# Attention's steps in TensorE's hand-written order begin at S5 block 3's transposes in place of block 1's

## The chip, the cores and the metric

The kernel runs as one launch on one core of a Trainium2 chip. The metric is the device time of one execution in microseconds (us); three executions of the kernel before took 1083.37, 1087.34 and 1088.72 us, median 1087.34. About 0.5% is what a measurement of this kernel can tell from no change.

## The reference, cut to what matters

One encoder layer over 2048 tokens of width 1024. A combined input projection feeds two mixers that run side by side:

```python
proj = x @ s5_w_in                          # 512 columns for S5, 256 for the queries
mix = _s5_mixer(proj[..., :512], ...)       # 32 groups of 16 channels, 64 complex states each,
                                            # a scan over tokens forward and one backward,
                                            # y -> g = gelu(y) -> g * sigmoid(g @ w_glu + b_glu)
mem_out = _memory_attention(proj[..., -256:], mem, w_kv)   # 4 heads of 64, 256 memory tokens, softmax
y = concat([mix, mem_out]) @ w_out
x = LN(alpha * x + y);  x = LN(alpha * x + MoE(x))          # 16 experts, 2 per token
```

The change is in the stretch where the S5 outputs and the attention over the memory tokens are computed; the GLU (`g @ w_glu`) follows, then the output projection, then the mixture of experts.

## The kernel before, in words

**Stages.** `front` computes the projections (`inproj_u`), then the S5 scans and outputs and the attention, then `glu`, then `outproj`; `moe` follows. Tokens are treated in 16 tiles of 128. The 32 S5 groups are treated in 8 blocks of four; the scans of the blocks run in the order 6, 7, 0, 1, 2, 3, 4, 5, mostly on VectorE and GpSimd (`turn_states`, L690 to L695, and the scan itself, L715), and ScalarE copies a scanned block into `SS` (L720).

**The S5 outputs.** `s5_out(b)` does for block b four groups of eight float32 matmuls each: `U` against `M` (L802, L803), `SS` against `wol` (L804, L805). Two groups share one PSUM tile `py`, which ScalarE copies to `gt` (L807). `M` and `wol` are loaded through SP's queue for each pair of groups (L789, L796). After every odd block come four sets of four transposes (`trg`, L816) of two blocks' outputs; each set fills a PSUM tile and is passed through `gelu`: ScalarE Square (L824), VectorE (L825), ScalarE Tanh (L826), VectorE (L827), the last of which writes `gT` (named S in the rows) and is the last reader of the `trg` tile. `py` and `trg` share one ring of three PSUM tiles (pool `ps1`, tag "s5"); `gu`, the scratch of `gelu`, has two buffers.

**The attention.** `attention_steps` is a generator of 57 steps: in round n (0 to 18) it does `att_values(n - 3)`, `att_probs(n - 2)` and `att_scores(n)`, where these tiles exist, one per step. `att_scores` is eight matmuls into `pS` (two PSUM tiles, L734, L735), a maximum on VectorE (`nm`, L737), four exponentials on ScalarE into `pe` (L740), a reciprocal (L742) and a multiply on GpSimd (L743). `att_probs` transposes `pe` (L757) and splits it into `th` (ScalarE, L758) and `tl` (VectorE, L759). `att_values` is 24 small matmuls (L773). The SBUF pool of `pe` (`attw`) is opened where the pool of the scans' scratch tiles `R` and `m` was closed before, and the pool of the GLU's `gh` and `gl` is opened where `attw` was closed: a tile waits until the last user of the memory beneath it is done.

**The order on TensorE.** Around the S5 outputs TensorE's order is that of the program (`manual_schedule`); the order on the other engines is planned by the framework. `s5_out` yields ahead of each group and ahead of each set of transposes, 48 times in all: blocks 0, 2, 4, 6 four times, blocks 1, 3, 5, 7 eight times (four groups, four sets). At each yield the next number of `STEPS` says how many attention steps are issued there:

```python
with self.tc.manual_schedule(engines={mybir.EngineType.PE}):
    counts = iter(STEPS)
    for b in range(NB):
        if b == GELU:
            self.glu_weights()
        for _ in self.s5_out(b, gtp, wp, gup):
            for _ in range(next(counts)):
                next(steps, None)
    for _ in steps:
        pass
```

Before, `STEPS` is `(0,) * 8 + (1,) + (2,) * 39`: none at the groups of blocks 0 and 1, one at the first set of transposes behind block 1, two at every yield after that until the 57 steps are used up, which is in block 6.

Of the kernel before, what the change touches and what calls it, by code (L numbers as in the profile page):

```python
# [50 lines left out]
SPLIT = 1024  # L51
WHOLE_T = 12
BATCHES = ((0, 4), (4, 4), (8, 2), (10, 2), (12, 2), (14, 2))
STEPS = (0,) * 8 + (1,) + (2,) * 39
ATL = (2, 3)
WIP = 3
LW = 4
# [15 lines left out]
class Kern:  # L73
# [97 lines left out]
    def front(self, fr):  # L171
# [17 lines left out]
        with ExitStack() as s5:  # L189
# [9 lines left out]
            with ExitStack() as t2:  # L199
# [17 lines left out]
# [3 lines that stand above are left out]
# [1387 lines left out]
```

## Time and profile before

| what | value |
|---|---|
| median of three executions | 1087.34 us |
| the profiled execution | 1077.7 us |
| its span in the trace | 1075.9 us |
| TensorE matmul busy | 896.7 us (83%) |
| VectorE busy | 825.0 us (77%) |
| ScalarE busy | 540.8 us (50%) |
| GpSimd busy | 537.4 us (50%) |
| mean granted TensorE clock | 0.931 |
| TensorE busy in 440 to 490 us (GLU) | 48.66 of 50 us |
| TensorE busy in 490 to 520 us (output projection's start) | 29.48 of 30 us |

A profile page gives the share of busy time of each engine over the span, and the trace gives each instruction with its start, its duration and what ended the idle time ahead of it. Times in the rows are microseconds from the start of the span. PE is TensorE, DVE VectorE, ACT ScalarE, POOL GpSimd, SP the queue that issues most transfers. PEclk 1.00 is the upper of TensorE's two clock levels (2.4 GHz), 0.50 the lower (1.2 GHz). The stretch of the change reaches from about 290 to 440 us of the span; the GLU's first matmul (tile `pg`) starts at 440.12.

### The profile page before, as it was taken

To read this page: it belongs to the slowest core of one execution; us is meant where nothing else is said; L and a number is where in the kernel's file an instruction comes from. 1 tells how busy PE (TensorE), PEld (TensorE's weight loads), DVE (VectorE), ACT (ScalarE), POOL (GpSimd) and SP (SyncE) were. 2 spreads that over 40 slices of the span, in tenths; PEclk is the share of its full clock that TensorE was granted. 3 is DMA by queue.
4 is the path that set the end of the run, shared out by engine and by line. 5 is a ranking of instruction groups with operands and counts; after the bars stand their busy time and mean duration, and the time that the engine had idled before them with its cause. 6 is when DMAs were issued, how large, how long until landed. Compare 5 with 4: busy or idle time off the path is not lost. (4 is left out here: it accounts for less than half of the span.)

```text
span 1075.9 us, 18762 instructions
## 1 busy us (share of the span) xinstructions
PE 896.7 (83%) x7108; PEld 607.8 (56%) x7108; DVE 825.0 (77%) x1636; ACT 540.8 (50%) x1068; POOL 537.4 (50%) x379
## 2 busy tenths in 40 slices
PE   7778599986754999899999988599959996988980
PEld 4445465675643777444555557486647664755640
DVE  7999988969997676384486866379858787978874
ACT  5122253445748777477743421366636564745530
POOL 1475755426664332324946364524544566357554
PEclk9899899999886999999999996899989999999995
DMA  7113355275171422326755341675568669658431
GB/s 258 40 44 119 122 181 200 70 234 188 48 226 43 154 80 80 120 77 244 252 177 80 121 116 62 246 294 192 199 239 306 214 227 341 216 193 286 170 96 66
DMA packets 65198, 178.14 MB, mean 166 GB/s; under 512 B 15120, under 2 KB 33424, under 8 KB 57680
## 3 DMA queue, kind: packets, MB, share of 16 engines
q1 hardware_dynamic: 44800, 128.83, 36.5%
q0 software_dynamic: 20304, 48.07, 12.9%
q8 instruction: 57, 0.93, 0.4%
q14 instruction: 37, 0.30, 0.1%
HBM read 141.95 MB, written 58.49 MB: 186 GB/s over the span
## 5 line engine op out<-in xcount | busy, mean ns | idle before, releaser
L92 DVE SCALAR_TENSOR_TENSOR wl<-raw,wh 128x1024 f16<-128x1024 f32 x82 | 97.7, 1219 | 10.1 <-ACT wh L91 10.1
L91 ACT ACTIVATE wh<-raw 128x1024 f16<-128x1024 f32 x82 | 82.0, 1048 | 23.3 <-PE pg L109 12.2
L109 PE MATMUL pg<-xl,wh 128*128 128x288 f16 (+1 forms) x256 | 72.4, 285 | 5.1 <-DVE xl L1477 4.4
L108 PE MATMUL pg<-xh,wh 128*128 128x288 f16 (+1 forms) x256 | 72.8, 286 | 2.9 <-ACT xh L1476 1.8
L1221 POOL DMA_INDIRECT xs<-xg,idxall x31 | 39.4, 1272 | 71.4 <-DVE xg L1514 41.9
L108 PE MATMUL pu<-xh,wh 128*128 128x288 f16 (+1 forms) x256 | 72.1, 284 | 1.9 <-DVE hl L1063 1.9
L110 PE MATMUL pg<-xh,wl 128*128 128x288 f16 (+1 forms) x256 | 72.1, 284 | 0.5 <-issue 0.5
L110 PE MATMUL pu<-xh,wl 128*128 128x288 f16 (+1 forms) x256 | 72.0, 284 | 0.0
L109 PE MATMUL pu<-xl,wh 128*128 128x288 f16 (+1 forms) x256 | 71.9, 284 | 0.0
L109 PEld LDWEIGHTS <-wh 128*128 128x128 f16 x576 | 58.1, 101 | 20.6 <-issue 7.1
L110 PEld LDWEIGHTS <-wl 128*128 128x128 f16 x576 | 57.9, 101 | 20.0 <-issue 6.8
L108 PEld LDWEIGHTS <-wh 128*128 128x128 f16 x576 | 58.0, 101 | 19.4 <-issue 4.6
L108 PE MATMUL pq<-xh,S 128*128 128x128 f16 x256 | 50.1, 233 | 15.9 <-DVE OT L295 15.9
L743 POOL TENSOR_TENSOR pe<-pe,ri 128x1024 f32<-128x1024 f32 x16 | 30.3, 1895 | 54.5 <-DVE ri L742 40.6
L108 PE MATMUL py<-wh,hh 128*128 128x512 f16 x120 | 45.9, 384 | 13.2 <-DVE xg L1514 10.1
L1216 POOL DMA_INDIRECT xg<-x1d,idxall x31 | 39.2, 1266 | 32.6 <-DMA out_x<-xg,idxall 14.5
L108 PE MATMUL pu<-winh,xh 128*128 128x512 f16 x128 | 49.7, 389 | 6.7 <-ACT winh L91 6.6
L691 POOL TENSOR_TENSOR m<-S,R 128x1024 f32<-128x1024 f32 x10 | 31.4, 3144 | 41.7 <-DVE S L715 23.6
L110 PE MATMUL pq<-xh,S 128*128 128x128 f16 x256 | 50.3, 233 | 0.0
L109 PE MATMUL pq<-xl,S 128*128 128x128 f16 x256 | 50.1, 233 | 0.0
L1477 DVE TENSOR_TENSOR xl<-pt,xh 128x512 f16<-128x512 f32 x60 | 39.5, 682 | 13.6 <-ACT xh L1476 8.4
L109 PE MATMUL pu<-winl,xh 128*128 128x512 f16 x128 | 49.4, 386 | 0.3 <-DVE winl L92 0.3
(471 smaller groups left out, 3134.1 us busy)
## 6 DMA issues: line engine op xcount, KB each, us to landing
raw<-in_w_gate SPq DMA_DIRECT2D x16, 1024.0 KB
raw<-in_w_up SPq DMA_DIRECT2D x16, 1024.0 KB
raw<-in_w_down SPq DMA_DIRECT2D x16, 1024.0 KB
xr<-in_xT SPq DMA_DIRECT2D x16, 512.0 KB
xs<-wo SPq DMA_DIRECT2D x16, 512.0 KB
wol<-xs SPq DMA_DIRECT2D x16, 512.0 KB
M<-kd SPq DMA_DIRECT2D x64, 128.0 KB
xres<-in_x SPq DMA_DIRECT2D x16, 512.0 KB
```

The costliest lines, as they stand in the source:

```text
L91: self.nc.scalar.activation(hi, raw, AF.Copy, scale=WS)
L92: self.nc.vector.scalar_tensor_tensor(lo, raw, WS, hi, op0=ALU.mult, op1=ALU.subtract)
L108: mm(ps, lh, rh, start=first, stop=False)
L109: mm(ps, lh, rl, start=False, stop=False)
L110: return mm(ps, ll, rh, start=False, stop=last)
L691: Q.tensor_tensor(m[:, 1], S[:, :, 1::-1], tab(1), op=ALU.mult)
L743: nc.gpsimd.tensor_tensor(pe, pe, ri.unsqueeze(2).to_broadcast([P, 4, 256]), op=ALU.mult)
L1216: return self.nc.gpsimd.indirect_dma_start(out=out, out_offset=None, in_=src, in_offset=bass.IndirectOffsetOnAxis(ap=idx, axis=0))
L1221: st = self.nc.gpsimd.indirect_dma_start(out=self.xs, out_offset=bass.IndirectOffsetOnAxis(ap=si, axis=0), in_=z[:sz], in_offset=None, bou ...
L1477: nc.vector.tensor_tensor(xl[:, ds_, :n], pt, xh[:, ds_, :n], op=ALU.subtract)
```

## The change: when the attention's steps are issued

One constant is changed:

```diff
-STEPS = (0,) * 8 + (1,) + (2,) * 39
+STEPS = (0,) * 20 + (2,) * 28
```

Now no attention step is issued at the first 20 yields, which are the groups of blocks 0 to 3 and the transposes behind block 1. From the first set of transposes behind block 3 on, two steps are issued at each of the 28 yields that are left, 56 in all; the 57th step is empty. The last step with work in it (`att_values(15)`) stands ahead of the last set of transposes behind block 7. No instruction, transfer or buffer is added or removed.

## Rows read from the trace of the kernel before

**Rows 1.** Windows of the stretch: engines' busy time (instructions), granted clock, DMA share, GB/s

```profile
335.30:342.07 6.77, 6.03 (x28) 4.52 (x28) 5.86 (x11) 6.77 (x21) 1.89 (x1) 0.56 0.00 0
342.07:369.24 27.17, 26.88 (x259) 22.56 (x257) 17.84 (x35) 19.58 (x62) 11.20 (x6) 1.00 0.38 118
369.24:381.44 12.20, 9.75 (x129) 8.17 (x128) 9.91 (x20) 10.76 (x34) 3.96 (x3) 1.00 0.29 86
381.44:411.00 29.56, 28.66 (x275) 24.25 (x274) 19.37 (x38) 21.47 (x68) 11.25 (x6) 1.00 0.36 109
411.00:421.35 10.35, 8.05 (x114) 6.66 (x113) 7.75 (x14) 8.03 (x22) 2.02 (x2) 1.00 0.35 102
421.35:435.30 13.95, 13.95 (x66) 11.97 (x64) 6.08 (x11) 6.42 (x12) 0.00 (x0) 1.00 0.00 1
435.30:440.12 4.82, 2.06 (x17) 1.71 (x17) 2.57 (x4) 3.47 (x7) 0.00 (x0) 1.00 0.72 263
440.12:443.60 3.48, 3.48 (x11) 1.33 (x10) 3.31 (x6) 2.96 (x7) 0.00 (x0) 0.52 0.67 235
```

**Rows 2.** Waits of TensorE, 310 to 445: us in total, times, longest

```profile
PE pS L734 <- ACT pe L740: 15.4, 2, 15.0
```

**Rows 3.** Timeline of TensorE: start, us, instruction, idle before and what ended it

```profile
315.77 1.11 PE L816 MATMUL trg<-ident,gt 128*128 128x128 f32 x4 [4.67 <-ACT gt L807]
316.67 0.42 PE L734 MATMUL pS<-kh,OT 128*128 128x256 f16 x1
...
318.38 1.91 PE L816 MATMUL trg<-ident,gt 128*128 128x128 f32 x8
335.32 0.37 PE L734 MATMUL pS<-kh,OT 128*128 128x256 f16 x1 [15.02 <-ACT pe L740]
...
436.01 1.53 PE L816 MATMUL trg<-ident,gt 128*128 128x128 f32 x12 [0.69 <-ACT gt L807]
439.61 0.63 PE L816 MATMUL trg<-ident,gt 128*128 128x128 f32 x4 [2.07 <-DVE S L827]
```

**Rows 4.** Timeline of SP's queue: the last load for block 3

```profile
315.54 3.72 SPq L796 DMA_DIRECT2D M<-kd  x4
```

**Rows 5.** Timeline of ScalarE around TensorE's long wait

```profile
312.91 1.70 ACT L720 ACTIVATE SS<-S 64x256 f32<-64x256 f32 x4
...
326.90 1.05 ACT L824 ACTIVATE gu<-trg 128x512 f32<-128x512 f32 x2
328.43 0.63 ACT L826 ACTIVATE gu<-gu 128x512 f32<-128x512 f32 x1 [0.48 <-DVE gu L825]
330.82 3.41 ACT L720 ACTIVATE SS<-S 64x256 f32<-64x256 f32 x8 [1.76 <-DVE S L695]
```

**Rows 6.** Timeline of VectorE in the same stretch

```profile
327.71 0.68 DVE L825 SCALAR_TENSOR_TENSOR gu<-gu,trg 128x512 f32<-128x512 f32 x1
330.04 0.69 DVE L695 TENSOR_TENSOR S<-S 128x512 f32<-128x512 f32 x1 [1.64 <-POOL S L691]
330.64 1.28 DVE L737 TENSOR_REDUCE nm<-pS 128x2 f32<-128x512 f32 x2
331.84 0.68 DVE L825 SCALAR_TENSOR_TENSOR gu<-gu,trg 128x512 f32<-128x512 f32 x1
332.44 0.68 DVE L827 SCALAR_TENSOR_TENSOR S<-gu,trg 128x512 f32<-128x512 f32 x1
```

**Rows 7.** Timelines of VectorE and GpSimd: the chain of the last token tile's scores

```profile
411.60 1.29 DVE L737 TENSOR_REDUCE nm<-pS 128x2 f32<-128x512 f32 x2 [0.62 <-PE pS L735]
...
414.76 1.90 POOL L743 TENSOR_TENSOR pe<-pe,ri 128x1024 f32<-128x1024 f32 x1 [3.64 <-PE trg L816]
```

**Rows 8.** Waits of SP's queue, 412 to 440

```profile
SPq L846 <- PE pT L757: 5.3, 1, 5.3
```

**Rows 9.** Timelines of ScalarE and VectorE: the GLU's casts, the last gelu parts

```profile
421.76 3.21 ACT L853 ACTIVATE gh<-S 128x512 f16<-128x512 f32 x6
...
442.60 1.47 DVE L827 SCALAR_TENSOR_TENSOR S<-gu,trg 128x512 f32<-128x512 f32 x2
```

## The prediction, made before the changed kernel ran

> **What bounds the kernel now.** I read the page's busy shares first, then its 40 slices, then the waits of TensorE between 310 and 445 us, then timelines and windows of that stretch. TensorE is the busiest engine over the span, and it is nearly full in the GLU and the start of the output projection behind this stretch (table of the profile), so a delay or a gain at the GLU's first matmul should reach the end one for one; I assume that. The page's chain of waits stops at the last store and tells nothing of this stretch.
>
> The stretch itself has one large hole: TensorE waits 15.0 us for ScalarE's exponentials [rows 2]. The timeline shows what stands there: three sets of transposes behind block 1 and the scores of token tile 0 are issued by 320.3, and the scores of tile 1 follow at 335.32 [rows 3]. Those scores need a `pS` tile that tile 0's exponentials empty, and these write `pe`, whose memory lies under the scans' scratch; they start behind the last copies of a scanned block, which run from 330.82 to 334.23 [rows 5]. From 342.07 on TensorE is dense: 26.88 us busy of 27.17 while groups and attention alternate, and 13.95 of 13.95 when the last eight groups run alone [rows 1]. The two stretches with transposes and attention side by side are looser (9.75 of 12.20, 8.05 of 10.35) [rows 1].
>
> **What the change moves.** Nothing is added or taken away; TensorE's queue is reordered. What it would have to win is the 15 us hole, by the eight groups of blocks 2 and 3, which at full clock take as long as the last eight groups, 13.95 us [rows 1]. Their data are there: SP issues the last load for block 3 at 315.54 [rows 4], and the copies of block 3's states are done at 314.61 [rows 5].
>
> *The wait.* But between the transposes behind block 1 and block 2 lies the ring of three PSUM tiles. Three sets of transposes fill it. The fourth set needs the first set's `gelu` finished, the first pair of block 2's groups needs the second set's. The same situation stands in the trace behind block 7, with no attention near it: three sets go out, the fourth waits 2.07 us for VectorE's L827 [rows 3]. Behind block 1 that `gelu` is late, since ScalarE and VectorE are in the middle of the last scans: the Squares run at 326.90, the first L825 at 327.71, the first Tanh at 328.43, the first L827 only at 332.44 [rows 5, 6]. The changed kernel leaves this in place. Following the traced order with the attention's maxima (1.28 us at 330.64) taken out, VectorE does the last scan piece to 330.7, the second L825 to 331.4, the first L827 to 332.0. The fourth set goes out there. The second Tanh then stands behind the eight copies on ScalarE (to 334.23), and the second L827 ends about 0.6 + 0.7 us later, at 335.5. So block 2 starts at 335.5, and TensorE's restart is +0.2 us against 335.3. Other end: if the planner puts the second L825 and Tanh ahead of the scan's last piece, the chain of four parts of 0.6 to 0.7 us each that begins with the first Squares (326.90) lets block 2 start at 330.8, 4.7 us earlier. I take 335.5, since this is the order that the trace has.
>
> By the Trainium skill (Perfetto Trace Analysis, Optimizing Tensor Performance, Matmuls) independent matmul groups should rotate through PSUM banks so that one group's evacuation lies beside the next group's matmuls. By that rule the groups of blocks 2 and 3 would fill the hole, which is the first rival below; the trace has the rotation already, and all three tiles are held.
>
> *The segments.* I cut TensorE's order at the yields and price each part of the new order by the segment of before with the same content [rows 1].
> - Blocks 2 and 3, eight groups alone: 13.95 us, plus the low clock at the restart. The restart of before ran 6.77 us at 0.56, a loss of 6.77 × 0.44 = 3.0 us. Together 16.95; 335.5 becomes 352.45.
> - The four sets behind block 3 with the attention's first steps: a new situation, since the pipeline of the attention has to fill. Scores 0 go out some 1.2 us after the last group (0.69 for the evacuation [rows 3], one set 0.5). Their chain through maxima, exponentials and the multiply takes 414.76 + 1.90 - 411.60 = 5.1 us [rows 7]. One Square and one Tanh (0.5 to 0.6 each) compete with it on ScalarE: 1.2. Then the transposes of tile 0's probabilities and the last set, 0.9 + 0.5; with 0.5 for the first half of the scores, 9.4 us, to 361.85. Lower end: work alone, four sets of 0.5, two scores, one set of probabilities, 4.6 us. Upper end: the 12.20 of transposes with full attention.
> - Blocks 4 and 5 with attention: 29.56 (same content), to 391.4.
> - The sets behind block 5 with full attention: 12.20, to 403.6.
> - Blocks 6 and 7 with attention: 29.56, to 433.2.
> - The sets behind block 7 with the attention's tail: 10.35 less one token tile's scores, which fall one yield earlier. Eight score matmuls take 318.38 - 316.67 = 1.7 us at the low clock [rows 3], half of it at full: 0.86. So 9.5, to 442.7.
>
> Before, the corresponding point is 440.12.
>
> *The GLU's start.* `gh` and `gl` lie in the attention's memory: the small load for the GLU at the same place in the pool waits 5.3 us on SP for the last transposes of `pe` [rows 8]. Before, six `gh` casts ran at 421.76, under the last groups, and cost TensorE nothing [rows 9]. That cover is gone: they come after `att_probs(15)`, some 3 us ahead of TensorE's last set, and queue with the last `th` copies and `gelu` parts. I charge 0.7 us, between 0 and 4.6 (they stand behind all remaining `gelu` parts, which before ended at 444.07 [rows 9], 4 us after the last set, and a cast of 0.6). Loads queued behind that small one on SP (the output projection's weights) start later too; they are needed behind the whole GLU.
>
> *The clock.* Before, the GLU's first 3.48 us ran at 0.52, behind a stretch in which TensorE was busy 2.06 of 4.82 us; behind the attention's tail (8.05 of 10.35) it stayed at 1.00 [rows 1]. So the GLU would start at the upper level: -3.48 × 0.48 = -1.7. The filling behind block 3 (some 4.6 of 9.4 busy) looks like the former case; I charge the same +1.7 for a fall there, between 0 and the 3.0 of the restart.
>
> Sum: 442.7 + 0.7 - 440.1 - 1.7 + 1.7 = +3.3 us. The profiled execution took 1077.7 us (span 1075.9, 1.8 around it), so its like would take 1081.0. It lies 9.6 below the median of the three runs; carried to the median, 1087.34 + 3.3 = 1090.6.
>
> **The rivals.**
> - *The hole is filled.* The first `gelu` parts are planned ahead of the scans' rest and the ring never blocks: blocks 2 and 3 run from 319.9. They end at 319.9 + 16.95 = 336.9, which is behind the moment (334.23) when `pe` is free; with the same segments and the 0.7 the GLU starts at 336.9 + 9.4 + 29.56 + 12.20 + 29.56 + 9.5 + 0.7 = 427.8, 12.3 earlier than before, the two clock terms cancelling: 1075.0. For it: loads and states are ready. Against it: rows 5 and 6, where ScalarE's queue holds the Squares until 326.90 although the transposes end near 317.
> - *Half of that.* Block 2 starts at 330.8: 3.3 - 4.7 = -1.4, 1085.9. For it: VectorE idles 1.64 us ahead of the scan's last piece [rows 6], room for the second L825.
> - *The GLU waits for its casts (slower).* Place: ScalarE behind `att_probs(15)`. If the planner lets the last four `gelu` chains go ahead of the first `gh`, the GLU starts 4.6 in place of 0.7 us behind the last set, and in that idle time the clock falls as before (+1.7): 3.3 + 3.9 + 1.7 = +8.9, 1096.2. It decides from the point where the first `gh` is later than the last set of transposes by more than 2 us. For it: before, in the same place, two `gh` stood among the `gelu` parts; against it: five of these parts' inputs come later than the memory of `pe`.
> - *No effect to see:* the order moves idle time from one place to another, 1087.3. It lies inside the forecast's own range.
>
> **How the numbers follow.** The forecast 0.54, hole filled 0.10, half of it 0.18, late casts 0.18. 0.5% of the median is 5.4 us. The forecast's own range is 1084 to 1095 (fill 4.6 to 12.2 us, clock 0 to 3.0, the runs' own spread of 1083.4 to 1088.7); of its 0.54 some 0.12 lies over +5.4. Half the hole gives mostly no change, 0.03 of it faster by over 0.5%. Late casts give slower in 0.14 of 0.18. So faster 0.14, same 0.60, slower 0.26. The range to hold the time 8 times in 10 is 1080 to 1097.5: it leaves out the filled hole and the far end of the late casts.
>
> **What would show it.** Right: TensorE idle from about 319.5, with a short set near 332, until 333 to 336, and the wait there put down to VectorE's L827; L802 of block 2 at about 335.5; a filling of some 9 us near 352 with waits for `pe`; the GLU's first matmul at 441 to 445 at full clock. Wrong: L802 of block 2 before 325 (the ring did not block), a hole under 8 us, or a `gh` cast later than 445. It would also be wrong if the gain or loss at the GLU's start does not reappear at the end of the span.

## The result, and the profile after

The changed kernel takes 1092.2 us (median of 16 runs, 1082.1 to 1099.6), the kernel before 1085.28 beside it (16 runs). The ratio is 1.0081 with a 95% interval of [1.0059, 1.0104]: slower by some 8.8 us (the two medians lie 6.9 us apart, inside that interval). The profiled execution of after took 1082.1 us (span 1080.3), the lowest of its runs, so its span stands only 4.4 us above that of before. The place where the time goes is read from inside the span.

TensorE's waits in 310 to 500 us of after (us in total, times, longest), three rows of the view:

```profile
PE trg L816 <- DVE S L827: 13.5, 1, 13.5
PE pg L108 <- ACT sg L862: 6.2, 2, 6.0
...
PE py L802 <- issue: 2.6, 1, 2.6
```

The row for the GLU in before:

```profile
PE pg L108 <- ACT sg L862: 1.3, 2, 0.8
```

The hole behind block 1 is still there, under another name: [rows 2] had 15.0 us for the exponentials, now 13.5 us stand for the last reader of a `trg` tile. The second row lies inside the GLU and has grown from 1.3 to 6.2 us. TensorE's timeline of after has both places:

```profile
317.10 2.82 PE L816 MATMUL trg<-ident,gt 128*128 128x128 f32 x12 [5.42 <-ACT gt L807]
333.39 1.08 PE L816 MATMUL trg<-ident,gt 128*128 128x128 f32 x4 [13.47 <-DVE S L827]
337.03 1.19 PE L802 MATMUL py<-M,U 128*128 128x256 f32 x2 [2.55 <-issue]
...
444.75 0.38 PE L108 MATMUL pg<-gh,E 128*128 128x512 f16 x1 [1.22 <-DVE bglu L847]
...
466.80 0.58 PE L108 MATMUL pg<-gh,E 128*128 128x512 f16 x1 [5.99 <-ACT sg L862]
```

Windows of after, cut where the prediction cut (us, then busy us and instructions of PE, PEld, DVE, ACT, POOL, then the granted clock, DMA share and GB/s); they answer to [rows 1]. The two dense segments of groups with attention, 29.30 and 28.50 us, are left out:

```profile
337.00:353.13 16.13, 16.10 (x64) 13.55 (x64) 4.91 (x8) 5.67 (x10) 0.00 (x0) 0.87 0.47 129
353.13:363.90 10.77, 7.06 (x42) 5.96 (x42) 7.26 (x13) 8.68 (x25) 3.42 (x2) 0.74 0.65 196
393.20:406.30 13.10, 10.40 (x124) 9.28 (x119) 10.20 (x21) 11.76 (x36) 5.68 (x3) 0.87 0.26 83
434.80:444.70 9.90, 7.23 (x105) 5.82 (x104) 7.86 (x17) 8.38 (x22) 1.89 (x1) 1.00 0.20 57
466.80:470.60 3.80, 3.80 (x10) 1.29 (x10) 2.65 (x3) 2.70 (x5) 3.72 (x2) 0.50 0.06 23
```

The GLU reaches from 444.75 to 495.1, 50.4 us; before it reached from 440.12 to 484.7, 44.6 us. So of the 10.4 us by which its end is late, 4.6 come from the attention's stretch and 5.8 arise in the GLU. These are readings of one execution each. In the four traces that share the order of before up to the GLU (before, e5, e8 and e10 below) it starts at 440.1 to 442.0, in the four that share the order of after (after, e1, e2, e7) at 443.1 to 445.4: 3.0 us later in the mean.

ScalarE's queue in the GLU of after (L102 and L91 are the casts `owh` of the six `w_out` chunks for the output projection, L862 is the GLU's Tanh, which empties a `pg` tile):

```profile
443.78 3.74 ACT L853 ACTIVATE gh<-S 128x512 f16<-128x512 f32 x7
...
448.41 1.05 ACT L102 ACTIVATE owh<-oraw 128x1024 f16<-128x1024 f32 x1
...
456.03 1.06 ACT L102 ACTIVATE owh<-oraw 128x1024 f16<-128x1024 f32 x1 [5.11 <-DMA oraw<-in_w_out]
458.92 1.06 ACT L91 ACTIVATE owh<-oraw 128x1024 f16<-128x1024 f32 x1 [1.83 <-DMA oraw<-in_w_out]
465.12 1.06 ACT L102 ACTIVATE owh<-oraw 128x1024 f16<-128x1024 f32 x1 [5.14 <-DMA oraw<-in_w_out]
466.08 0.67 ACT L862 ACTIVATE sg<-pg,bglu 128x512 f32<-128x512 f32 x1
```

The same queue before:

```profile
443.25 1.04 ACT L102 ACTIVATE owh<-oraw 128x1024 f16<-128x1024 f32 x1
...
450.69 1.06 ACT L102 ACTIVATE owh<-oraw 128x1024 f16<-128x1024 f32 x1 [5.44 <-DMA oraw<-in_w_out]
453.55 1.06 ACT L91 ACTIVATE owh<-oraw 128x1024 f16<-128x1024 f32 x1 [1.80 <-DMA oraw<-in_w_out]
454.52 1.25 ACT L862 ACTIVATE sg<-pg,bglu 128x512 f32<-128x512 f32 x2
...
461.57 1.04 ACT L102 ACTIVATE owh<-oraw 128x1024 f16<-128x1024 f32 x1
```

Two things differ. The first cast runs at 448.41 in place of 443.25. Most of these 5.2 us are the GLU's own later start: against it the cast comes 3.7 us later in after and 3.1 us in before. The later casts follow at the same distances (the third 7.6 us behind the first, before 7.4), since the chunks share two buffers and a later load waits for the split of an earlier chunk. And the planner has put the fifth cast ahead of the first Tanh; before, two Tanhs, two `mh` and four `gh` stood ahead of it and it waited for nothing. So the first Tanh runs at 466.08 in place of 454.52.

SP's queue, first after (its wait at the bias load, then the `w_out` loads behind it), then before:

```profile
SPq L846 <- PE pT L757: 45.4, 1, 45.4
```

```profile
440.87 3.02 SPq L923 DMA_DIRECT2D oraw<-in_w_out  x2
...
452.09 11.48 SPq L923 DMA_DIRECT2D oraw<-in_w_out  x4
```

```profile
436.22 21.98 SPq L923 DMA_DIRECT2D oraw<-in_w_out  x6
```

### The profile page after: what moved, and what is told of

It is laid out like the page before. It is cut to its first block, busy times and chain, and to the rows that moved or that the text cites. A ratio compares the mean times of both kernels' runs of the same rounds, so it can differ in the third digit from the quotient of the medians.

```text
span 1080.3 us, 18761 instructions
## 1 busy us (share of the span) xinstructions
PE 899.1 (83%) x7108; PEld 610.7 (57%) x7108; DVE 826.7 (77%) x1636; ACT 542.0 (50%) x1068; POOL 539.8 (50%) x379
## 5 line engine op out<-in xcount | busy, mean ns | idle before, releaser
L91 ACT ACTIVATE wh<-raw 128x1024 f16<-128x1024 f32 x82 | 81.6, 1048 | 18.4 <-PE pg L109 6.9
L108 PE MATMUL pq<-xh,S 128*128 128x128 f16 x256 | 51.5, 236 | 15.9 <-DVE OT L295 15.9
L1476 ACT ACTIVATE xh<-pt 128x512 f16<-128x512 f32 x60 | 34.6, 592 | 40.8 <-PE pt L1473 39.7
L691 POOL TENSOR_TENSOR m<-S,R 128x1024 f32<-128x1024 f32 x10 | 34.0, 3403 | 41.8 <-DVE S L715 23.6
L1473 PE MATMUL pt<-ident,xg 128*128 128x128 f32 x240 | 39.3, 287 | 15.9 <-DMA xg<-x1d,idxall 10.6
L110 PE MATMUL pq<-xh,S 128*128 128x128 f16 x256 | 51.6, 236 | 0.1
L1514 DVE SCALAR_TENSOR_TENSOR xg<-py,idxall,xg 128x512 f32<-128x512 f32 x60 | 43.5, 745 | 10.5 <-DMA xg<-xs,idxall 6.6
```

The costliest lines, as they stand in the source:

```text
L91: self.nc.scalar.activation(hi, raw, AF.Copy, scale=WS)
L108: mm(ps, lh, rh, start=first, stop=False)
L110: return mm(ps, ll, rh, start=False, stop=last)
L691: Q.tensor_tensor(m[:, 1], S[:, :, 1::-1], tab(1), op=ALU.mult)
L1473: nc.tensor.transpose(pt[:, i, off:off + sz], x[:sz, (d0 + i) * P:(d0 + i) * P + P], self.ident[:sz, :sz])
L1476: nc.scalar.activation(xh[:, ds_, :n], pt, AF.Copy)
```

## The experiments

Each was timed in five rounds against the kernel before on the same chip, with 12 executions of the changed version (9 of e1, 6 of e7). The GLU's first and last matmul, the longest wait of TensorE for `sg` there, and the start of the first gather of the mixture of experts (tile `xk`) come from one profiled execution each. In the cuts of code, `...` marks what is left out:

| kernel | GLU | wait for `sg` | `xk` | ratio to before, 95% |
|---|---|---|---|---|
| before | 440.1 to 484.7 | 0.8 | 647.4 | 1 |
| after | 444.7 to 495.1 | 6.0 | 656.8 | 1.0081 [1.0059, 1.0104] |
| e1 bias early | 443.1 to 493.2 | 5.9 | 657.0 | 1.0067 [1.0043, 1.0091] |
| e2 casts behind | 445.4 to 487.0 | none | 651.7 | 1.0005 [0.9979, 1.0031] |
| e3 sets late | 441.8 to 484.6 | none | 647.0 | 0.9984 [0.9958, 1.0009] |
| e4 from block 2 | 447.4 to 491.5 | none | 653.5 | 1.0047 [1.0017, 1.0077] |
| e5 loads held | 441.5 to 488.7 | 2.7 | 650.6 | 1.0018 [0.9990, 1.0046] |
| e6 sets late, other steps | 441.6 to 484.8 | none | 646.7 | 0.9974 [0.9948, 1.0000] |
| e7 two casts | 443.1 to 494.3 | 7.3 | 655.9 | 1.0120 [1.0080, 1.0159] |
| e8 fifth ahead | 442.0 to 490.5 | 3.8 | 653.6 | 1.0040 [1.0012, 1.0067] |
| e9 e6 with e2's edit | 441.1 to 484.6 | none | 649.5 | 1.0015 [0.9990, 1.0041] |
| e10 before with e2's edit | 440.8 to 482.0 | none | 645.1 | 1.0003 [0.9975, 1.0030] |

The theories: *order* (ScalarE's planned order puts a cast that waits for its load ahead of a Tanh) against *late loads* (the GLU's small bias load holds SP's queue, 45.4 us in after, until the last transposes of `pe` free the attention's memory, and the `w_out` loads behind it come too late), and *late start* (the loss is the GLU's later start and the move itself).

**e1, the bias loaded early** (after, the bias in memory of its own, so that it holds no queue):

```diff
+self.bg = self.const.tile([P, 4], F32, name="bglu")   # ahead of the attention
+nc.sync.dma_start(self.bg, a["b_glu"])
...
-bg = kp.tile([P, 4], F32, bufs=1, name="bglu")       # in the GLU
-nc.sync.dma_start(bg, a["b_glu"])
```

> The changed kernel with the GLU's bias (bglu) in a tile of its own, loaded long before the attention; nothing else differs. In the changed kernel SP's queue stands 45 us at the bias load, whose memory the attention's pe holds, and the six loads of w_out start behind it at 440.9. Theory 'late loads': these loads now start near 436, ScalarE's casts of w_out come some 4 to 5 us earlier, the 6.0 us wait of the GLU's matmuls for the sg Tanh shrinks to under 2 us, and the time falls by 4 to 6 us against the changed kernel, to a ratio of about 1.003 to 1.004 against the kernel before. Rival 'order': the wait comes from ScalarE's planned order (the fifth w_out cast ahead of the first Tanh), which this kernel keeps; then the wait stays at 5 us or more and the ratio near 1.008. Rival 'attention's tail': the loss is all ahead of the GLU; then the wait shrinks and the ratio stays.

The first `w_out` load now goes out at 433.69 in place of 440.87; the second still waits for a set of transposes, until 441.93 (443.56 in after). The wait for `sg` stays at 5.9 us. ScalarE's timeline of e1 still begins the casts only behind the `gh`, and the fifth still stands ahead of the first Tanh:

```profile
446.74 1.05 ACT L102 ACTIVATE owh<-oraw 128x1024 f16<-128x1024 f32 x1
...
463.27 1.06 ACT L102 ACTIVATE owh<-oraw 128x1024 f16<-128x1024 f32 x1 [5.20 <-DMA oraw<-in_w_out]
464.23 0.67 ACT L863 ACTIVATE sg<-pg,bglu 128x512 f32<-128x512 f32 x1
```

The bias load that holds the queue is not the cause of the wait. A version of after with all of its loads early was not tried.

**e2, the casts behind** (after, all six `w_out` casts on ScalarE behind the fourth Tanh of the GLU's first block):

```diff
+if t == 0:                                # the GLU's first block
+    self.tanh0 = tanh.ins                 # overwritten at each Tanh: the fourth stays
...
-(self.split_w_q if c in OWQ else self.split_w)(wh[:, c], wl[:, c], raw)
+with self.tc.issue_after(self.tanh0):
+    (self.split_w_q if c in OWQ else self.split_w)(wh[:, c], wl[:, c], raw)
```

> The changed kernel with ScalarE's casts of w_out queued behind the fourth Tanh of the GLU's first token block; SP's queue is as in the changed kernel, the bias load still holds it. Both 'late loads' and 'order' expect the 6.0 us wait of the GLU's matmuls for sg to go: GLU end some 6 to 8 us earlier than in the changed kernel, ratio 1.000 to 1.003 against the kernel before, provided that the casts are done before the output projection starts. 'Attention's tail' expects no change from 1.008.

The first Tanhs of e2 run as soon as TensorE has written their tiles, and the first casts follow without a wait:

```profile
454.35 1.33 ACT L862 ACTIVATE sg<-pg,bglu 128x512 f32<-128x512 f32 x2 [3.58 <-PE pg L110]
...
460.78 1.05 ACT L102 ACTIVATE owh<-oraw 128x1024 f16<-128x1024 f32 x1
```

The GLU takes 41.6 us and the loss is gone within the interval, although it starts at 445.4. Against after that is some 8 us by the ratios, 8.1 us at the GLU's end and 5.1 us at `xk`. So the casts ahead of the Tanhs cause the wait in the GLU, and *late start* falls as the only cause. That the later start costs nothing does not follow: this GLU is also 3.0 us shorter than that of before, so the edit wins back more than the 5.8 us that the GLU had lost. Against before, e2 lies between -2.3 and +3.4 us by the interval, +4.3 by `xk` of the one profiled execution. The pair for the later start is e2 and e10, below.

**e8, the fifth cast ahead** (before, one order edge more: the fifth cast ahead of the first Tanh) and **e5, the loads held** (before, the `w_out` loads behind a small store that reads what the second set behind block 7 writes to `gT`, so that they start at 441.83). They put the two differences into the kernel before one at a time (the lines are shortened):

```diff
+self.tc.add_manual_dep(self.tanh0, self.cast.name, NoSync)      # e8: c == 4
...
+self.hold = nc.sync.dma_start(hold, self.gT[:, 3, 1020:1024])   # e5
+with self.tc.issue_after(self.hold): nc.sync.dma_start(raw, a["w_out"][:, c])
```

> The kernel before (STEPS as before) with one thing of the changed kernel's plan put in: on ScalarE the fifth cast of w_out stands ahead of the GLU's first Tanh. Theory 'order': the Tanh comes at about 461 in place of 454.5, the GLU's matmuls wait 4 to 6 us for it (1.3 us before) with the clock falling behind the wait, the time is 4 to 8 us longer, ratio 1.004 to 1.008 against the kernel before. Rival 'late chain': without the late start of the loads the fifth cast costs little, wait under 3 us, ratio under 1.003.

> The kernel before with one thing of the changed kernel put in: the six loads of w_out stand on SP's queue behind a 2 KB store of gT's columns of the second set behind block 7, which ends near 440, so that they start at 440 to 442 instead of 436.2. ScalarE's planned order is that of the kernel before, attention ends at 421 as before. 'Late loads' expects the GLU's matmuls to wait 4 to 6 us for the sg Tanh (1.3 us before) and the time 3 to 6 us longer, ratio 1.003 to 1.006. 'Order' expects no wait over 2 us and a ratio within 0.999 to 1.002, since here the fifth cast stays behind the first two Tanhs.

ScalarE in e8:

```profile
445.15 1.04 ACT L102 ACTIVATE owh<-oraw 128x1024 f16<-128x1024 f32 x1
...
461.58 1.06 ACT L102 ACTIVATE owh<-oraw 128x1024 f16<-128x1024 f32 x1 [3.06 <-DMA oraw<-in_w_out]
462.55 1.25 ACT L862 ACTIVATE sg<-pg,bglu 128x512 f32<-128x512 f32 x2
```

ScalarE in e5:

```profile
447.01 1.06 ACT L102 ACTIVATE owh<-oraw 128x1024 f16<-128x1024 f32 x1 [2.31 <-DMA oraw<-in_w_out]
...
458.12 1.25 ACT L864 ACTIVATE sg<-pg,bglu 128x512 f32<-128x512 f32 x2
...
465.18 1.04 ACT L102 ACTIVATE owh<-oraw 128x1024 f16<-128x1024 f32 x1
```

The order alone costs 0.40% (4.3 us, clear of zero). In e8 the planner has also moved four `gh` ahead of the fifth cast. Later casts alone cost 0.18% (2 us, an interval that holds zero), with a wait of 2.7 us that lies between the two theories. The two shares do not simply add up to the loss of after: in e5 the first cast runs 5.5 us behind the GLU's start, in after only 3.7. In the GLU's length the order alone makes 3.9 us (48.5 against 44.6) of the 5.8 that after has more.

**e7, two casts** (after, only the fifth and sixth cast behind the second Tanh, which is `tanh1`):

```diff
+with self.tc.issue_after(self.tanh1) if c > 3 else ExitStack():
     (self.split_w_q if c in OWQ else self.split_w)(wh[:, c], wl[:, c], raw)
```

> The changed kernel with only the fifth and sixth casts of w_out queued behind the second Tanh of the GLU on ScalarE, which is about the place that they have in the kernel before; the bias load still holds SP's queue and the gh casts still come behind the attention. Theory 'order': the GLU's matmuls wait under 2.5 us for sg (6.0 in the changed kernel, 1.3 before), the GLU ends 5 to 7 us earlier than in the changed kernel, ratio 1.000 to 1.004 against the kernel before. Rival 'late chain' (the first w_out casts and gh casts are late by 4 to 5 us whatever the order): the wait stays over 4 us, ratio 1.005 to 1.008.

A miss: it is no better than after. Its ratio is higher, but over six executions, and the two intervals overlap. The two casts went right behind the second Tanh and ahead of the third, for which TensorE waits 7.3 us:

```profile
458.01 1.25 ACT L862 ACTIVATE sg<-pg,bglu 128x512 f32<-128x512 f32 x2
463.24 1.06 ACT L102 ACTIVATE owh<-oraw 128x1024 f16<-128x1024 f32 x1 [3.98 <-DMA oraw<-in_w_out]
...
470.91 0.69 ACT L862 ACTIVATE sg<-pg,bglu 128x512 f32<-128x512 f32 x1 [0.71 <-DVE ml L867]
```

So the price does not hang on the fifth cast and the first Tanh alone: here the same kind of wait stands ahead of the third.

**e4, from block 2** (after, one constant): do the steps cost less when they begin eight groups earlier, at block 2's first?

```diff
-STEPS = (0,) * 20 + (2,) * 28
+STEPS = (0,) * 12 + (2,) * 36
```

> The changed constant with the attention's first step at block 2's first group, two per yield, so that the attention ends at block 7's first group and not at its last set; nothing else differs. TensorE's queue reaches block 2 behind the same blocked ring, at about 336. The planned order on ScalarE in the GLU is close to that of the kernel before (the fifth cast behind three Tanhs). Theory 'order': the GLU's matmuls wait under 2.5 us for sg, and the first of them comes at 440 to 443, ratio 1.000 to 1.004. If the start of the attention as such were what costs, the ratio would lie between 1.004 and 1.008.

A miss in place and in size: the GLU starts at 447.4, not at 440 to 443. TensorE's waits of e4:

```profile
PE trg L816 <- DVE S L827: 17.2, 2, 15.2
PE pg L108 <- DVE S L827: 3.1, 1, 3.1
```

The hole stays as long as the sets stand behind block 1, and 3.1 us of a last set's `gelu` come ahead of the GLU. Its `sg` wait is gone though no cast was touched: the fifth cast stands behind the first Tanhs again, so ScalarE's order shifts with the steps.

**e3, the sets late** (the sets of block 1 behind the groups of blocks 2 and 3, with a second `gt` tile): this removes the ring as the cause of the hole.

```diff
-STEPS = (0,) * 20 + (2,) * 28
+STEPS = (0,) * 16 + (2,) * 32
...
+self.late.append((b, gt))              # behind an odd block
+if b == 1:
+    return
+for b, gt, t4 in [(b, gt, t4) for b, gt in self.late for t4 in range(4)]: ...
```

> The changed kernel with block 1's four sets of transposes moved behind the groups of blocks 2 and 3 (ahead of block 3's own sets), a second tile for gt, and the attention's steps from the first of these sets on. Theory 'ring': what kept blocks 2 and 3 out of the 13.5 us hole is the ring of three PSUM tiles held by the sets whose gelu waits for the scans. Then block 2's groups start at 312 to 316, blocks 2 and 3 end near 330, the hole shrinks to under 6 us, and the GLU's first matmul comes at 428 to 434 (440.1 before): 6 to 12 us faster than the kernel before less up to 6 us for the GLU's wait, ratio 0.990 to 0.998. Rival: the groups wait for their own data (scanned states, M, wol) or for ScalarE's evacuation behind the scans; then the hole is only cut into pieces and the ratio is 1.003 to 1.008.

TensorE of e3:

```profile
313.85 0.70 PE L804 MATMUL py<-M,U 128*128 128x256 f32 x2 [3.29 <-ACT gt L809]
...
328.43 0.70 PE L804 MATMUL py<-M,U 128*128 128x256 f32 x2 [3.95 <-ACT gt L809]
...
335.81 1.11 PE L821 MATMUL trg<-ident,gt 128*128 128x128 f32 x4 [1.98 <-ACT gt L809]
```

Blocks 2 and 3 run in what was the hole, cut into pieces by ScalarE's copies (the waits for `gt`). With the waits of after for L827 this shows that the ring had held them. But the GLU starts at 441.8, not at 428 to 434. **e6** gives the steps otherwise, one at a set and three at a group:

```diff
-STEPS = (0,) * 16 + (2,) * 32
+STEPS = (0,) * 16 + (1,) * 8 + (3,) * 8 + (1,) * 4 + (3,) * 8 + (1,) * 4
```

> The kernel with block 1's sets of transposes behind the groups of blocks 2 and 3, with the attention's 57 steps spread by what stands beside them: one per set of transposes, three per group of blocks 4 to 7, so that the attention ends ahead of block 7's sets. Theory 'pace' (with two steps at every yield the filled hole was given back, since the last groups ran with attention beside them and the sets with attention are bound by ScalarE and VectorE, 12 us for four): the GLU's first matmul comes at 430 to 436 (441.8 with two steps everywhere, 440.1 in the kernel before), ratio 0.991 to 0.996. Rival 'floor' (ScalarE's and VectorE's work on the attention sets the pace whatever the order): the first matmul stays at 438 to 443, ratio 0.997 to 1.001.

Again 441.6. TensorE's wait of e6 that took the place:

```profile
PE trg L821 <- DVE S L832: 15.2, 5, 7.3
```

Where before eight groups ran alone at the end, 13.95 us [rows 1], the eight sets in a row now wait for `gelu`, and the last groups have attention between them. With either set of steps the gain of the filled hole is given back ahead of the GLU; that it is a floor of ScalarE and VectorE was not tried. e6 is the fastest of all, but its interval touches 1.

**e9, e6 with e2's edit, and e10, before with e2's edit**:

> The late sets (block 1's sets behind blocks 2 and 3, steps as in e6) and the w_out casts behind the fourth Tanh together. If the two edits act in different places and add up, the GLU starts at 441 to 443 as in e6, runs in 41.6 to 42.5 us in place of 43.2, and the ratio to the kernel before is 0.994 to 0.997. Rival: e6 has no cast ahead of a Tanh that waits, so there is nothing left to take, 0.997 to 0.999.

> The kernel before with all six w_out casts behind the fourth Tanh of the GLU's first block. If ScalarE's order costs the GLU something in the kernel before too (44.6 us against 41.6 in e2), the GLU ends near 481.7 and the ratio is 0.996 to 0.999. Rival: in the kernel before, the two Tanhs that stand first already cover the loads, and only the later part of the GLU differs between the executions: 1.000, GLU 44 to 45 us.

Both are misses; neither wins. In e10 the GLU takes 41.2 in place of 44.6 us. Half of that is not the edit's doing: TensorE's work ahead of the GLU is the same as in before (2.24 us busy of the last 5.00 in both), yet the clock did not fall this time. The GLU's first 3.48 us ran at 1.00, in before at 0.52 [rows 1], a difference of 1.7 us:

```profile
440.81:444.29 3.48, 3.48 (x19) 1.59 (x18) 3.32 (x6) 2.71 (x6) 0.00 (x0) 1.00 0.65 239
```

The output projection's first matmul then waits 1.5 us for ScalarE, and the ratio is 1.0003; a gain of the 2.3 us that `xk` shows lies just inside the interval. In e9 there was no Tanh behind a waiting cast to free, and the edit adds the same wait of 1.5 us.

e2 and e10 have the same edit and the GLU at 1.00 throughout, and differ in the attention's steps alone. The GLU of e2 starts 4.6 us later and ends 5.0 us later, and `xk` comes 6.6 us later. The ratios, 1.0005 and 1.0003, show no difference, with some 3 us to either side of each. So what the later start alone costs is not settled: between nothing and some 6 us.

So no version beats the kernel before by more than can be measured.

## Why the prediction was right in its range and where it failed

Its steps against the trace of after, in the order of the sum:

| step | predicted | trace of after |
|---|---|---|
| fourth set behind block 1 | 332.0 | 333.39 |
| block 2's first group | 335.5 | 337.03 |
| end of blocks 2 and 3 | 352.45 | 353.13 |
| sets behind block 3, with the fall of the clock | 9.4 + 1.7 = 11.1 | 10.77, clock 0.74 |
| blocks 4 and 5 | 29.56 | 29.30 |
| sets behind block 5 | 12.20 | 13.10 |
| blocks 6 and 7 | 29.56 | 28.50 |
| sets behind block 7, with the tail | 9.5 | 8.7 (434.8 to 443.5) |
| to the GLU's first matmul | 0.7 | 1.2 |
| GLU's first matmul | 443.4 + 1.7 = 445.1 | 444.75 |
| length of the GLU | 44.6 - 1.7 = 42.9 | 50.4 |

**What held.** The ring blocks TensorE behind block 1. The fourth set waits for the first L827, and block 2's first group starts at 337.03, right behind the end of the second L827 at 336.93 (the profile names no releaser for that wait and calls it "issue"). The first Tanh of `gelu` runs at 329.75, but the second is at 335.58, behind eight copies of the scan, as the prediction took over from [rows 5, 6]; ScalarE and VectorE of after:

```profile
332.14 3.41 ACT L720 ACTIVATE SS<-S 64x256 f32<-64x256 f32 x8 [1.77 <-DVE S L695]
335.58 0.63 ACT L826 ACTIVATE gu<-gu 128x512 f32<-128x512 f32 x1
```

```profile
332.56 0.68 DVE L827 SCALAR_TENSOR_TENSOR S<-gu,trg 128x512 f32<-128x512 f32 x1
...
336.24 0.69 DVE L827 SCALAR_TENSOR_TENSOR S<-gu,trg 128x512 f32<-128x512 f32 x1 [3.00 <-ACT gu L826]
```

Some 1.3 us of the lateness arise ahead of the change: the sets go out at 317.10, before at 315.77 [rows 3]. All segments together miss the GLU's start by 0.35 us, which is partly luck: block 2 comes 1.5 us late, the segments behind it are 1.9 us shorter than predicted, and the four traces with this order spread over 2.3 us. The clock at the GLU's start is 1.00, as predicted; the 0.87 in the sets behind block 5 was not. That the change raised it is not shown: with the order of before the GLU's first 3.48 us ran at 0.52 (before), 0.54 (e8) and 0.63 (e5), but at 1.00 in e10.

**What failed.** The step that reads "Loads queued behind that small one on SP (the output projection's weights) start later too; they are needed behind the whole GLU". What they feed, the output projection, is indeed late enough. But the casts between stand in ScalarE's queue, and the Tanhs of the GLU stand behind them. The term was priced at nothing; the GLU's length misses by 7.5 us (50.4 against 42.9), and e2, which takes these casts (with the rest of each chunk's split) out of the way, wins it back. In parts: TensorE's waits for `sg` are 6.2 us in place of 1.3, and behind the wait the clock falls, 3.80 us at 0.50, a loss of 1.9; together 6.8 of the 7.5. The 1.7 us that the higher clock gained at the GLU's start are no gain here, since the first Tanh, and not TensorE, decides when the GLU goes on.

By the Trainium skill (PSUM — Partial Sum Buffer, Engine vs sequencer instructions) the queues of ScalarE, VectorE and GpSimd are strictly first in, first out. The traces agree: the Tanh whose tile TensorE had written by about 454 (454.35 in e2, where nothing stood ahead of it) ran at 466.08, behind a cast that waited 5.14 us. Read at the time, this rule asks of every late load which instructions stand behind its reader.

A second assumption failed with it and carries the larger part: that the order on the other engines stays as traced. The prediction knew that it is planned, and let it vary for `gh` and `gelu` only. The loads' lateness alone is small: against the GLU's start the first cast comes 0.5 us later than before, and e1 with its first load 7.2 us earlier keeps the wait. The order alone, in e8, makes 3.9 of the 5.8 us.

The assumption that a delay at the GLU's first matmul reaches the end one for one does not hold either. e3 and e6 start the GLU 1.6 us and 1.5 us later than before and end it within 0.1 us of it.

**The rivals.** "The GLU waits for its casts" named ScalarE at the GLU's start and +8.9 us, near what came; its mechanism did not come. The first `gh` runs at 443.78, behind TensorE's last set (442.87) by under 2 us, and the GLU starts 1.2 us behind that set's end. Five of the first eight `gh` start later than the 445 that the prediction gave as a sign against itself, the last at 447.89; TensorE waits for none of them, so the sign was badly chosen. The casts that cost the time were those of `w_out`. "The hole is filled" and its half fell with the 13.47 us in the trace, and e3 shows that a filled hole does not bring the GLU's start 12.3 us forward: it starts at 441.8, 1.6 us later than before.

**The numbers.** 1092.2 lies 1.6 above the 1090.6, inside the range; that is partly luck, since the kernel before came out 2.1 us lower in these runs. On the prediction's own 1087.34 the ratio would give 1096.1, at the edge of the range. By the ratio the change is +8.8 where +3.3 was predicted: the side was right, the likeliest class (within 0.5%) was not, as the whole interval lies above 1.005. Of the +3.3, the later start (+5.0) came out at +4.6 in the trace and the GLU's length (-1.7) at +5.8. Two slips in the working change nothing: the parts of the chances add to 0.13 faster and 0.61 the same, not 0.14 and 0.60, and of the transposes that "end near 317" only the first set does, the third ends at 320.3 [rows 3].

**What stays open**: why the planner put the fifth cast ahead of the first Tanh in after and not before. It is a planned order, and no run shows its costs. Open too is the price of the later start alone (e2 against e10).

## What to carry to other kernels

When a load comes later, price not only its last use but the first instruction that reads it, and list what stands behind that instruction in its engine's queue: an instruction that waits for a transfer holds all that follow. Where a planner writes the other engines' orders, treat a reordering on one engine as a reordering on all of them, and put a range on it. Work that fills an earlier hole is missing where it stood before: in e3 and e6 the eight groups that ran alone at the end, and the gain was given back ahead of the GLU.

## What the runs showed that was not expected

Behind a wait in the middle of the GLU the clock fell: the ten matmuls behind the 5.99 us in after ran at 0.50 for 3.80 us, those behind the 3.84 us in e8 for some 2.9 us, those behind the 2.66 us in e5 for some 2.6 us. In the sets behind block 7 of after, with TensorE busy 7.23 of 9.90 us between short gaps, the clock stayed at 1.00. And the same instructions need not give the same clock: with the same 2.24 us busy in the 5.00 us ahead of the GLU it started at 0.52 in before and at 1.00 in e10.

The time behind `xk`, which no edit touches, varied from 420.1 (e8, 653.6 to 1073.7) to 434.1 us (e9, 649.5 to 1083.6) over the profiled executions. So two profiled spans do not rank two kernels here. The marks ahead of it agree better with the timed ratios, but not closely: against before, `xk` and the ratio differ by up to 4.4 us (e7), the span and the ratio by up to 6.5 us (e8).
